# A two-layer hybrid trunk with eight experts: slot matrices made together, activations split per two blocks, the first expert weight tile split in the mixer

## The chip, the cores and the metric

The kernel runs on one core of a Trainium2 chip. The metric is the device time of one execution in microseconds (us). The engines that matter here are TensorE (PE, matmuls; PEld is its weight load), VectorE (DVE), ScalarE (ACT) and SyncE (SP), which issues the loads of weights. Each engine takes its instructions in the order in which they stand in its own list, and waits where an operand is not ready.

## What is computed

Two layers over 256 latent and 256 context tokens of width 1024. A layer is a norm, three parallel attention branches merged by gates, an output projection with a residual, a second norm and a feed-forward part. In layer 0 that is a dense SwiGLU; in layer 1 it is a mixture of eight experts of which each latent token uses two. Cut to the part that the change touches, with each token's rows gathered, passed through the expert and scattered back:

```python
def moe_swiglu(h, w_router, w_gu, w_dn):
    hf = h.reshape(n, D)
    logits = (hf @ w_router).astype(jnp.float32)
    top_logit, top_e = lax.top_k(logits, TOP_K)          # 2 of 8
    top_w = jax.nn.softmax(top_logit, axis=-1)
    ...
    xb = hf[src_tok].reshape(n_blocks, EXPERT_ROW_BLOCK, D)
    yb = lax.map(lambda a: swiglu(a[0], w_gu[a[1]], w_dn[a[1]]), (xb, block_expert))
    yb = yb.reshape(n_rows, D) * row_w[:, None].astype(h.dtype)
    return jax.ops.segment_sum(yb, src_tok, num_segments=n).reshape(B, L, D)

def swiglu(h, w_gu, w_dn):                               # w_gu: 1024 x 5632, w_dn: 2816 x 1024
    gate, up = jnp.split(h @ w_gu, 2, axis=-1)
    return (jax.nn.silu(gate) * up) @ w_dn
```

## The kernel before

All weights are fp32 in memory and are used as pairs of fp16: a tile `raw` of 128x2048 (1 MiB) is loaded by SP into a ring of raw buffers, ACT makes the high half (`wh<-raw`, line 269) and DVE the low half (`wl<-raw,wh`, line 266; `split`). Every product is three matmuls (high by high, high by low, low by high). The pairs live in a ring of three buffers (`WB = 3`, `new_parts`), so the split of a tile waits until the matmuls of the tile three places before have ended.

Each expert has room for 96 tokens (`CAP`) and 33 weight tiles. **Gate/up** are 22 of them, in 11 blocks `b` of two tiles: a tile is 48 matmuls of 96 columns (lines 332 to 334) into an accumulator `pa` (four buffers); behind a block ACT takes the Silu and DVE the product (`ht`, 128x192), which ACT and DVE split again (`hdh`, `hdl`). **Down** are the other 11 tiles: 44 steps `j` of three matmuls of 512 columns (lines 1300 to 1302) into `pg` (two buffers).

What an expert needs of the tokens is made by `gather`: from the slot numbers `posm` and weights `wsel` of the router, DVE makes a 0/1 matrix `P` (two instructions, line 1220), PE transposes it (line 1224; ACT copies it to `PT`, needed at the end to scatter), multiplies it by the weights (line 1228; DVE makes `wsl` of it, lines 1230 and 1231), and PE gathers the tokens' rows `hn` in 32 matmuls (line 1239, into two `pa` and two `pb` buffers), which ACT casts into `xg` (line 1241). Expert 0's is called in front of the experts; that of expert e+1 is called in the down phase of expert e (`j == 12`, `next_slots`). After experts 2, 5, 6 and 7 `combine` scatters the finished outputs back (line 1316) and DVE adds them to `xT`.

Ahead of the experts stands `route`: the second norm of layer 1, transposes of the normed tokens to `hn`, router logits, top 2, slots. The first three expert tiles are loaded early: tile 0 in the mixer's first part (into a buffer of the pool `px`), tiles 1 and 2 behind the mixer; the first two are split inside `route` (lines 1162 and 1203 for the high halves). The mixer's last part is the output projection (`out_chunk`): 8 chunks `d`, of which 0 to 3 are made for all latent tokens and 4 to 7 for each half of the tokens; behind each chunk DVE adds it to the residual `xT`, ACT squares it (`sq`) and DVE adds the squares (`acc`), whose sum over a half of the tokens starts the norm (lines 523 and 524).

The order on each engine comes from a scheduler that places instructions by dependences and its own times; `behind(...)` holds the instructions in its block back until the named ones have been issued on the same engine.

Of the kernel before, what the change touches and what calls it, by code (L numbers as in the profile page):

```python
# [17 lines left out]
D = 1024  # L18
KD = 8
NTOK = 512  # L20
NLAT = 256
# [228 lines left out]
def trunk(tc, A, out):  # L250
# [349 lines left out]
    def mixer(pool, i, ada_q, nrm, nxt, first=None):  # L600
# [444 lines left out]
        w = [W("wout2"), W("wout3")]  # L1045
        for p, c in enumerate(halves):
# [72 lines left out]
    ahead = [px.tile([128, 2048], FT, tag="raw3", bufs=1, name=nm("raw")) for _ in range(1)]  # L1119
# [20 lines left out]
    def route(pool):  # L1140
# [20 lines left out]
        with behind(nrm.end):  # L1161
            hi0 = S.activation(first[0][0], ahead[0], AF.Copy, scale=WS)
# [39 lines left out]
        with behind(e_):  # L1202
            S.activation(first[1][0], ahead[1], AF.Copy, scale=WS)
# [7 lines left out]
        with behind(V.tensor_tensor(wsel[:, :, :, 1], ex, wsel[:, :, :, 0], op=OP.subtract)):  # L1211
            for t in range(2):
                issued[0] = hi0, stt(first[t][1], ahead[t], WS, first[t][0], OP.mult, OP.subtract)

    def gather(pool, pos_e, w_e, slots):


        P = pool.tile([128, 2, CAP], F16, tag="P", bufs=2, name=nm("P"))
        for t in range(2):
            V.tensor_scalar(P[:, t], slots[:, :CAP], pos_e(t), None, op0=OP.is_equal)  # L1220
        PT = pool.tile([CAP, NLAT], F16, tag="PT", bufs=6, name=nm("PT"))
        pt = pb([128, D], F16)
        for t in range(2):
            T.transpose(pt[:CAP, 128 * t:128 * t + 128], P[:, t], ident16)
        S.copy(PT, pt[:CAP, :NLAT])
        pw = pb([128, 2])[:CAP]
        for t in range(2):
            T.matmul(pw, P[:, t], w_e(t), start=(t == 0), stop=(t == 1))
        wsl = pool.tile([CAP, 2], FT, tag="wsl", bufs=4, name=nm("wsl"))
        V.tensor_copy(wsl, pw)  # L1230
        V.tensor_scalar(wsl[:, 0:1], wsl[:, 0:1], wsl[:, 1:2], 1.0 / (WS * PSC), op0=OP.add, op1=OP.mult)
        xg = pool.tile([128, KD, 2, CAP], F16, tag="xg", bufs=2, name=nm("xg"))
        for j in range(2):
            for h in range(2):
                ps = (pb if h else pa)([128, 4, CAP])
                for k in range(4):
                    for t in range(2):
                        kk = 4 * h + k
                        T.matmul(ps[:, k], hn[j][:, t, 128 * kk:128 * kk + 128], P[:, t],  # L1239
                                 start=(t == 0), stop=(t == 1))  # L1240
                S.copy(xg[:, 4 * h:4 * h + 4, j], ps)
        return wsl, xg, PT

    def expert(pool, wsl, xg, tile_of, jobs, meanwhile, last=lambda *y: None, halves=(lambda *y: None,) * 2):
# [14 lines left out]
        for b in range(11):  # L1259
# [177 lines left out]
```

## Time and profile before

| | us |
|---|---|
| median of three executions | 1776.98 |
| lowest, highest | 1776.41, 1782.14 |
| the profiled execution | 1779.86 |
| its span, first to last instruction | 1777.8 |
| PE busy (share of the span) | 1649.0 (93%) |
| DVE busy | 1357.8 (76%) |
| ACT busy | 1040.6 (59%) |
| expert weight loads | 264 of 1 MiB |

The share of busy time is an average over parts with different limits: the experts are the last 700 us, and there DVE and ACT are far busier than the mean. A timeline row is: start, duration, engine, line, operation, output and inputs, and in brackets the idle time of the engine ahead of it and what ended that. The step from one start to the next tells the cost of an instruction better than its duration, since neighbours overlap. [...]

### The profile page before, as it was taken

Reading aid. Unit: us, or ns where it says so; the run is one execution under the profiler, and the core shown is the slowest. Engines: PE = TensorE matmul, PEld = TensorE weight load, DVE = VectorE, ACT = ScalarE, POOL = GpSimd, SP = SyncE. Lnnn points to the kernel's source line nnn. Section 1 sums busy time; section 2 is a strip of 40 time slices with the busy share of each in tenths; the row PEclk is TensorE's granted clock in tenths of the full one; section 3 lists DMA queues with packets and bytes.
Section 4 is the critical chain, followed back from the end, with each engine's and each line's share of the span. In section 5 each row is a group of like instructions: output and inputs, shape, how many; then the busy total and the mean of one; then the engine's idle time right before and its main releaser. Section 6 shows DMA issues by size and latency. Waiting matters only on the chain. (4 is left out here: it accounts for less than half of the span.)

```text
span 1777.8 us, 37905 instructions
## 1 busy us (share of the span) xinstructions
PE 1649.0 (93%) x16157; PEld 1086.9 (61%) x16157; DVE 1357.8 (76%) x1972; ACT 1040.6 (59%) x1399; POOL 1.3 (0%) x7
## 2 busy tenths in 40 slices
PE   5999899999999999999879988999899989998986
PEld 2554345446644444457646877686868686878684
DVE  4577656455886554547787779999989999989997
ACT  3456646343422322224666558888878888878785
POOL 0000000000000000000000000000000000000000
PEclk9999899999999999999988999999999999999998
DMA  9253488452365445534536669999999999999990
GB/s 388 101 153 88 109 250 225 134 192 96 138 224 207 168 161 177 182 112 159 160 84 158 194 262 366 416 410 410 417 400 385 408 422 408 418 387 396 390 391 26
DMA packets 149921, 451.94 MB, mean 254 GB/s; under 512 B 92144, under 2 KB 95344, under 8 KB 103024
## 3 DMA queue, kind: packets, MB, share of 16 engines
q1 hardware_dynamic: 148768, 448.50, 69.1%
q8 instruction: 128, 2.10, 0.5%
q10 hardware_dynamic: 976, 0.94, 0.2%
q14 instruction: 49, 0.40, 0.1%
HBM read 427.38 MB, written 1.05 MB: 241 GB/s over the span
## 5 line engine op out<-in xcount | busy, mean ns | idle before, releaser
L266 DVE SCALAR_TENSOR_TENSOR wl<-raw,wh 128x2048 f16<-128x2048 f32 (+1 forms) x476 | 820.5, 1735 | 52.7 <-ACT wh L269 50.7
L269 ACT ACTIVATE wh<-raw 128x2048 f16<-128x2048 f32 (+1 forms) x474 | 684.9, 1463 | 262.3 <-PE pa L333 92.6
L334 PEld LDWEIGHTS <-wl 128*128 128x128 f16 x4346 | 426.9, 98 | 183.0 <-DVE wl L266 66.9
L332 PEld LDWEIGHTS <-wh 128*128 128x128 f16 x4346 | 428.3, 99 | 131.3 <-issue 17.7
L333 PEld LDWEIGHTS <-wh 128*128 128x128 f16 x4346 | 427.4, 98 | 115.6 <-issue 8.7
L334 PE MATMUL pa<-xg,wl 128*128 128x96 f16 x2816 | 374.4, 207 | 42.9 <-DVE wl L266 42.9
L332 PE MATMUL pa<-xg,wh 128*128 128x96 f16 x2816 | 373.2, 206 | 1.0 <-ACT wh L269 1.0
L333 PE MATMUL pa<-xg,wh 128*128 128x96 f16 x2816 | 373.2, 206 | 0.1
L332 PE MATMUL pg<-hh,wh 128*128 128x512 f16 (+1 forms) x512 | 170.0, 332 | 5.7 <-ACT gt L972 2.7
L332 PE MATMUL pa<-hh,wh 128*128 128x512 f16 (+1 forms) x480 | 167.5, 355 | 6.1 <-ACT hh L552 6.1
L333 PE MATMUL pa<-hl,wh 128*128 128x512 f16 (+1 forms) x480 | 169.3, 354 | 1.3 <-DVE hl L266 1.3
L334 PE MATMUL pg<-hh,wl 128*128 128x512 f16 (+1 forms) x512 | 169.3, 331 | 0.7 <-DVE wl L266 0.7
L333 PE MATMUL pg<-hl,wh 128*128 128x512 f16 (+1 forms) x512 | 169.8, 332 | 0.0
L334 PE MATMUL pa<-hh,wl 128*128 128x512 f16 (+1 forms) x480 | 169.2, 353 | 0.0
L266 DVE SCALAR_TENSOR_TENSOR scr<-raw,cb 128x1024 f16<-128x1024 f32 x64 | 78.3, 1224 | 77.4 <-DMA raw<-in_ada 76.2
L1301 PE MATMUL pg<-wl,hdh 128*96 128x512 f16 x352 | 133.4, 379 | 1.0
L1302 PE MATMUL pg<-wh,hdl 128*96 128x512 f16 x352 | 133.4, 379 | 0.0
L1300 PE MATMUL pg<-wh,hdh 128*96 128x512 f16 x352 | 133.2, 379 | 0.0
L266 DVE SCALAR_TENSOR_TENSOR pn<-P,sml,pn 128x512 f16<-128x512 f32 (+1 forms) x96 | 60.9, 659 | 34.1 <-ACT pn L269 33.4
L269 ACT ACTIVATE pn<-P,sml 128x512 f16<-128x512 f32 (+1 forms) x96 | 59.1, 647 | 39.9 <-DMA pt<-pn 31.6
L913 ACT ACTIVATE P<-pa,sml 128x512 f32<-128x512 f32 (+1 forms) x96 | 58.1, 612 | 31.7 <-DVE sml L911 22.1
L269 ACT ACTIVATE hdh<-ht 128x192 f16<-128x192 f32 x88 | 31.9, 362 | 66.6 <-DVE ht L260 66.6
(250 smaller groups left out, 1919.3 us busy)
## 6 DMA issues: line engine op xcount, KB each, us to landing
raw<-in_wm SPq DMA_DIRECT2D x264, 1024.0 KB, 7.7
raw<-in_ws SPq DMA_DIRECT2D x52, 1024.0 KB, 4.8
raw<-in_ada SPq DMA_DIRECT2D x48, 1024.0 KB, 5.2
raw<-in_ws SPq DMA_DIRECT2D x18, 768.0 KB, 5.0
raw<-in_ws SPq DMA_DIRECT2D x16, 704.0 KB, 4.1
raw<-in_ws SPq DMA_DIRECT2D x16, 640.0 KB, 4.1
raw<-in_ws SPq DMA_DIRECT2D x4, 832.0 KB, 11.5
xT<-in_xt SPq DMA_DIRECT2D x4, 512.0 KB, 6.4
```

Source lines behind the costliest of these rows:

```text
L266: return V.scalar_tensor_tensor(o, a, s, b, op0=op0, op1=op1, **kw)
L269: h = S.activation(hi, src, AF.Copy, scale=scale)
L332: T.matmul(ps, sh, mh, start=first, stop=False)
L333: T.matmul(ps, sh, ml, start=False, stop=False)
L334: T.matmul(ps, sl, mh, start=False, stop=last)
L913: S.activation(P[t], ps[t], AF.Exp, bias=nb[:, t:t + 1], scale=sc, accum_out=sums[:, t:t + 1])
L1300: T.matmul(py, hdh[:, f], w[0][:, c], start=begin, stop=False)
L1301: T.matmul(py, hdh[:, f], w[1][:, c], start=False, stop=False)
L1302: T.matmul(py, hdl[:, f], w[0][:, c], start=False, stop=end)
```

## The change

Three things are changed. `gather` is divided: `slot_matrices` makes `P`, `PT` and `wsl`, first for expert 0 alone and then for experts 1 to 7 at once, held behind the low half of tile 2 (`behind(*lo)`); there are two DVE instructions of 128x672 for `P`, two copies for `PT` (96x1024 and 96x768) and one reduction with one scaling for `wsl`; what is left of `gather` is the 32 matmuls and the four casts, at the place of before. In the gate/up loop `ht` holds two blocks, and one split of 128x384 follows every second block; the eleventh block is split alone. The first expert tile is no longer loaded into a buffer of its own early in the layer; it is loaded and split in the mixer, after the loads of the output projection's last two tiles; the router then splits tiles 1 and 2, and tile 3 is loaded ahead as well. The ring of raw buffers keeps its size of twelve.

```diff
@@ mixer
         w = [W("wout2"), W("wout3")]
+        if last:
+            presplit.append(split_w(load_raw("wm", 0), 2048, step=2048))
         for p, c in enumerate(halves):
             for d in range(4, 8):
                 out_chunk(w[d // 2 - 2], d, c)
...
-    ahead = [px.tile([128, 2048], FT, tag="raw3", bufs=1, name=nm("raw")) for _ in range(1)]
+    presplit = []
@@ route
-            hi0 = S.activation(first[0][0], ahead[0], AF.Copy, scale=WS)
+            hi0 = S.activation(presplit[1][0], ahead[0], AF.Copy, scale=WS)
...
-            S.activation(first[1][0], ahead[1], AF.Copy, scale=WS)
+            S.activation(presplit[2][0], ahead[1], AF.Copy, scale=WS)
...
             for t in range(2):
-                issued[0] = hi0, stt(first[t][1], ahead[t], WS, first[t][0], OP.mult, OP.subtract)
-
-    def gather(pool, pos_e, w_e, slots):
-
-
-        P = pool.tile([128, 2, CAP], F16, tag="P", bufs=2, name=nm("P"))
+                lo[:] = [stt(presplit[1 + t][1], ahead[t], WS, presplit[1 + t][0], OP.mult, OP.subtract)]
+            issued[0] = hi0, lo[0]
+
+    def slot_matrices(pool, es, pos, w, slots):
+
+
+        n = len(es)
+        P = pool.tile([128, 2, n, CAP], F16, tag=f"P{n}", bufs=1, name=nm("P"))
         for t in range(2):
-            V.tensor_scalar(P[:, t], slots[:, :CAP], pos_e(t), None, op0=OP.is_equal)
-        PT = pool.tile([CAP, NLAT], F16, tag="PT", bufs=6, name=nm("PT"))
-        pt = pb([128, D], F16)
-        for t in range(2):
-            T.transpose(pt[:CAP, 128 * t:128 * t + 128], P[:, t], ident16)
-        S.copy(PT, pt[:CAP, :NLAT])
-        pw = pb([128, 2])[:CAP]
-        for t in range(2):
-            T.matmul(pw, P[:, t], w_e(t), start=(t == 0), stop=(t == 1))
-        wsl = pool.tile([CAP, 2], FT, tag="wsl", bufs=4, name=nm("wsl"))
-        V.tensor_copy(wsl, pw)
-        V.tensor_scalar(wsl[:, 0:1], wsl[:, 0:1], wsl[:, 1:2], 1.0 / (WS * PSC), op0=OP.add, op1=OP.mult)
+            sh = [128, n, CAP]
+            V.tensor_tensor(P[:, t], slots[:, None, :CAP].to_broadcast(sh), pos(t)[:, :, None].to_broadcast(sh),
+                            op=OP.is_equal)
+        PT = pool.tile([CAP, n, NLAT], F16, tag=f"PT{n}", bufs=1, name=nm("PT"))
+        for a in range(0, n, 4):
+            m = min(4, n - a)
+            pt = pb([128, 4, NLAT], F16)
+            for e in range(m):
+                for t in range(2):
+                    T.transpose(pt[:CAP, e, 128 * t:128 * t + 128], P[:, t, a + e], ident16)
+            S.copy(PT[:, a:a + m], pt[:CAP, :m])
+        pw = pb([128, n, 2])[:CAP]
+        for e in range(n):
+            for t in range(2):
+                T.matmul(pw[:, e], P[:, t, e], w(t)[:, e, :], start=(t == 0), stop=(t == 1))
+        wsl = pool.tile([CAP, n], FT, tag=f"wsl{n}", bufs=1, name=nm("wsl"))
+        V.tensor_reduce(wsl, pw, axis=AX.X, op=OP.add)
+        V.tensor_scalar(wsl, wsl, 1.0 / (WS * PSC), None, op0=OP.mult)
+        return [(wsl[:, e:e + 1], PT[:, e], lambda t, e=e: P[:, t, e]) for e in range(n)]
+
+    def gather(pool, P):
+
         xg = pool.tile([128, KD, 2, CAP], F16, tag="xg", bufs=2, name=nm("xg"))
...
@@ expert
-            t_ = pool.tile([128, 2, CAP], FT, tag="ht", bufs=3, name=nm("ht"))
+            if b % 2 == 0:
+                t4 = pool.tile([128, 4, CAP], FT, tag="ht", bufs=2, name=nm("ht"))
+            t_ = t4[:, 2 * (b % 2):2 * (b % 2) + 2]
             S.activation(t_, ps[:, :, 0], AF.Silu, scale=US)
-            f = slice(2 * b, 2 * b + 2)
             mul(t_, t_, ps[:, :, 1])
-            later.append(lambda f=f, t_=t_: split(hdh[:, f], hdl[:, f], t_, US * AS))
+            if b % 2 or b == 10:
+                n, f = 2 + 2 * (b % 2), slice(2 * b - 2 * (b % 2), 2 * b + 2)
+                later.append(lambda n=n, f=f, t4=t4: split(hdh[:, f], hdl[:, f], t4[:, :n], US * AS))
@@ the experts
-        raw_slots.extend([(px, "raw3", 1), (mr, "raw2", 5)])
-        ahead = ahead + [new_raw() for _ in range(2)]
...
+        raw_slots.append((mr, "raw2", 6))
+        ahead = [load_raw("wm", t * 128 * 2048) for t in range(1, 4)]
...
         with behind(issued[0][0]):
-            g = slots_of(0)
+            slots = matrices(0, 1)
+            xg = gather(pool, slots[0][2])
+        with behind(*lo):
+            slots += matrices(1, NE)
...
             def next_slots():
                 with behind(*issued[0]):
-                    return slots_of(e + 1)
+                    return gather(pool, slots[e + 1][2])
```

How this moves instructions is seen in the lists of three engines.

PE, the making of expert 2's inputs. Before, it stands in the down phase of expert 1, among the 512-column matmuls into `pg`; one row of each kind is shown, and 30 more gather matmuls (line 1239) follow ahead of the L1302:

```order
L1301 MATMUL pg_12877<-wl_12931,hdh_11613 96x512
L1224 LDWEIGHTS P_12934
L1224 MATMUL pb_12938<-ident_74,P_12934 96x128
L1228 LDWEIGHTS P_12934
L1228 MATMUL pb_12942<-wsel,P_12934 96x2
L1239 LDWEIGHTS hn_9835
L1239 MATMUL pa_12949<-P_12934,hn_9835 128x96
...
L1302 MATMUL pg_12877<-wh_12930,hdl_11614 96x512
```

After, half of it stands in expert 1's gate/up, among the 96-column matmuls into `pa` (the gathers are now on line 1253):

```order
L334 MATMUL pa_12301<-xg_11442,wl_12359 128x96
L332 LDWEIGHTS wh_12418
L332 MATMUL pa_12415<-xg_11442,wh_12418 128x96
L333 LDWEIGHTS wh_12418
L333 MATMUL pa_12415<-xg_11442,wh_12418 128x96
L1253 LDWEIGHTS hn_9840
L1253 MATMUL pb_12941<-P_10118,hn_9840 128x96
...
L1253 MATMUL pb_12961<-P_10118,hn_9841 128x96
L334 LDWEIGHTS wl_12419
L334 MATMUL pa_12415<-xg_11442,wl_12419 128x96
```

The run of 13 gather matmuls now stands right ahead of the first matmul of a tile that needs its low half (`wl`), and the transposes and slot weights are gone from both phases. By the whole list the down phases of experts 0 to 6 hold 32, 16, 0, 16, 16, 0 and 0 gather matmuls now (32 each before); those of experts 2 and 5 hold 16 of the matmuls that scatter (12 before).

DVE, gate/up of expert 0. Before, a product or a split of 192 columns stands behind every weight split:

```order
L266 SCALAR_TENSOR_TENSOR wl_10672<-raw_10669,wh_10671 128x2048
L260 TENSOR_TENSOR ht_10551<-ht_10551,pa_10440 128x192
L266 SCALAR_TENSOR_TENSOR wl_10726<-raw_10723,wh_10725 128x2048
L266 SCALAR_TENSOR_TENSOR hdl_10113<-ht_10551,hdh_10112 128x192
L266 SCALAR_TENSOR_TENSOR wl_10786<-raw_10783,wh_10785 128x2048
```

After, two products and one split of 384 columns stand among four weight splits:

```order
L266 SCALAR_TENSOR_TENSOR wl_10592<-raw_10589,wh_10591 128x2048
L260 TENSOR_TENSOR ht_10474<-ht_10474,pa_10363 128x192
L266 SCALAR_TENSOR_TENSOR wl_10646<-raw_10643,wh_10645 128x2048
L266 SCALAR_TENSOR_TENSOR wl_10706<-raw_10703,wh_10705 128x2048
L260 TENSOR_TENSOR ht_10474<-ht_10474,pa_10477 128x192
L266 SCALAR_TENSOR_TENSOR wl_10760<-raw_10757,wh_10759 128x2048
L266 SCALAR_TENSOR_TENSOR hdl_10159<-ht_10474,hdh_10158 128x384
```

One instruction in eight is gone, and none of the columns.

ACT, the end of the mixer and the start of expert 0. Before, the squares of the output projection's chunks follow one another, and at the start the cast of the last gathered piece stands behind the split of tile 2 (`raw_9849`):

```order
L508 ACTIVATE sq_9517<-xT 128x128
L508 ACTIVATE sq_9546<-xT 128x128
L508 ACTIVATE sq_9549<-xT 128x128
...
L1241 CAST xg_10071<-pb_10082 128x4x96
L269 ACTIVATE wh_10215<-raw_9849 128x2048
L1241 CAST xg_10071<-pb_10102 128x4x96
L269 ACTIVATE wh_10269<-raw_10267 128x2048
L269 ACTIVATE wh_10329<-raw_10327 128x2048
```

After, the split of tile 0 (`raw_9567`) stands ahead of the squares of chunk 3, and the casts stand together; `raw_9857` is tile 3, and the two copies of `PT` stand ahead of tile 4:

```order
L508 ACTIVATE sq_9516<-xT 128x128
L269 ACTIVATE wh_9569<-raw_9567 128x2048
L508 ACTIVATE sq_9545<-xT 128x128
...
L1254 CAST xg_10077<-pb_10088 128x4x96
L1254 CAST xg_10077<-pb_10108 128x4x96
L269 ACTIVATE wh_10309<-raw_9857 128x2048
L1234 COPY PT_10121<-pb_10122 96x1024
L1234 COPY PT_10121<-pb_10132 96x768
L269 ACTIVATE wh_10366<-raw_10364 128x2048
```

The low half of tile 0 moves on DVE in the same way, to in front of the sums of chunk 3's squares. On PE the first two of the 14 transposes of experts 1 to 7 stand behind the first matmul of tile 1, the other twelve 13 matmuls later, and the 14 slot-weight matmuls 30 behind those.

## Rows read from the trace of the kernel before

**Rows 1.** Stretches; busy PE, PEld, DVE, ACT, POOL; PE clock, DMA share, GB/s.

```profile
1054.00:1060.00 6.00, 4.37 (x48) 2.59 (x45) 5.42 (x28) 3.57 (x9) 0.00 (x0) 0.99 0.60 247
1060.00:1074.00 14.00, 8.16 (x94) 6.26 (x94) 12.11 (x45) 12.89 (x22) 0.00 (x0) 0.51 0.29 85
1150.00:1200.00 50.00, 45.87 (x851) 39.79 (x849) 49.08 (x37) 42.13 (x37) 0.00 (x0) 1.00 1.00 407
1200.00:1250.00 50.00, 48.45 (x571) 34.94 (x569) 47.03 (x35) 41.06 (x35) 0.00 (x0) 1.00 1.00 410
```

**Rows 2.** Waits, 1090 to 1730 us: total, times, longest.

```profile
PE pa L334 <- DVE wl L266: 42.1, 146, 0.9
ACT wh L269 <- PE pg L1302: 22.8, 30, 1.3
...
ACT wh L269 <- DMA raw<-in_wm: 9.7, 13, 1.0
```

**Rows 3.** SyncE's waits, 1090 to 1730 us; and its loads, from the page.

```profile
SPq L304 <- DVE wl L266: 205.1, 86, 4.0
...
raw<-in_wm SPq DMA_DIRECT2D x264, 1024.0 KB, 7.7
```

**Rows 4.** Timeline of DVE, gate/up of expert 1: start, duration, instruction.

```profile
1176.03 0.34 DVE L260 TENSOR_TENSOR ht<-ht,pa 128x192 f32<-128x192 f32 x1
1176.29 2.28 DVE L266 SCALAR_TENSOR_TENSOR wl<-raw,wh 128x2048 f16<-128x2048 f32 x1
1178.49 0.35 DVE L266 SCALAR_TENSOR_TENSOR hdl<-ht,hdh 128x192 f16<-128x192 f32 x1
1178.77 2.28 DVE L266 SCALAR_TENSOR_TENSOR wl<-raw,wh 128x2048 f16<-128x2048 f32 x1
```

**Rows 5.** Groups of DVE instructions by shape, from 1090 us on: busy, mean ns.

```profile
L260 DVE TENSOR_TENSOR raw<-raw,pb 128x512 f32<-128x512 f32 x4 | 2.5, 682 | 0.8 <-PE pb L533 0.8
```

**Rows 6.** Timeline of PE, gate/up of expert 1.

```profile
1175.70 0.21 PE L333 MATMUL pa<-xg,wh 128*128 128x96 f16 x1
1176.16 0.22 PE L334 MATMUL pa<-xg,wl 128*128 128x96 f16 x1 [0.26 <-DVE wl L266]
```

**Rows 7.** Timeline of PE, down phase of expert 1.

```profile
1220.95 0.38 PE L1301 MATMUL pg<-wl,hdh 128*96 128x512 f16 x1
...
1222.47 0.50 PE L1239 MATMUL pb<-P,hn 128*128 128x96 f16 x8
1222.81 0.38 PE L1302 MATMUL pg<-wh,hdl 128*96 128x512 f16 x1
```

**Rows 8.** Timeline of PE, down phase of expert 0.

```profile
1135.43 0.38 PE L1302 MATMUL pg<-wh,hdl 128*96 128x512 f16 x1
...
1136.98 0.38 PE L1300 MATMUL pg<-wh,hdh 128*96 128x512 f16 x1
...
1137.63 0.38 PE L1300 MATMUL pg<-wh,hdh 128*96 128x512 f16 x1
...
1139.08 0.38 PE L1301 MATMUL pg<-wl,hdh 128*96 128x512 f16 x1
```

**Rows 9.** Timeline of ACT, end of the mixer and start of expert 0.

```profile
1042.86 0.51 ACT L508 ACTIVATE sq<-xT 128x128 f32<-128x128 f32 x2 [1.09 <-DVE xT L266]
...
1073.14 1.91 ACT L269 ACTIVATE wh<-raw 128x2048 f16<-128x2048 f32 x1
1074.96 0.47 ACT L1241 CAST xg<-pb 128x384 f16<-128x384 f32 x1
1077.17 3.90 ACT L269 ACTIVATE wh<-raw 128x2048 f16<-128x2048 f32 x2 [1.74 <-issue]
```

**Rows 10.** Timeline of DVE, end of the mixer and start of expert 0.

```profile
1047.09 0.29 DVE L263 TENSOR_TENSOR acc<-acc,sq 128x128 f32<-128x128 f32 x1 [0.43 <-ACT sq L508]
...
1083.79 2.28 DVE L266 SCALAR_TENSOR_TENSOR wl<-raw,wh 128x2048 f16<-128x2048 f32 x1
```

**Rows 11.** Timeline of PE, end of the mixer.

```profile
1041.97 0.27 PE L334 MATMUL pa<-mh,wl 128*128 128x256 f16 x1
```

More of the change, by code (lines that the diff above doesn't have):

```diff
@@ L1238, in gather @@
                         kk = 4 * h + k
-                        T.matmul(ps[:, k], hn[j][:, t, 128 * kk:128 * kk + 128], P[:, t],
-                                 start=(t == 0), stop=(t == 1))
+                        T.matmul(ps[:, k], hn[j][:, t, 128 * kk:128 * kk + 128], P(t), start=(t == 0), stop=(t == 1))
                 S.copy(xg[:, 4 * h:4 * h + 4, j], ps)
-        return wsl, xg, PT
+        return xg
     def expert(pool, wsl, xg, tile_of, jobs, meanwhile, last=lambda *y: None, halves=(lambda *y: None,) * 2):
@@ L1339, in trunk @@
           tc.tile_pool(name="mr", bufs=1, reuse_waits="tile") as mr):
-        raw_slots.extend([(px, "raw3", 1), (mr, "raw2", 5)])
-        ahead = ahead + [new_raw() for _ in range(2)]
-        for t, raw in enumerate(ahead):
-            nc.sync.dma_start(raw, dram("wm", t * 128 * 2048, 2048))
-        first = [new_parts() for _ in range(2)]
-        route(pool)
+        raw_slots.append((mr, "raw2", 6))
+        ahead = [load_raw("wm", t * 128 * 2048) for t in range(1, 4)]
+        presplit.extend(new_parts() for _ in range(2))
+        lo = []
+        route(pool, lo)
         raw_slots.extend([(st, "hh", 1), (st, "hl", 1)])
@@ L1349, in moe_w, with matrices @@
         def moe_w(e, t):
-            if e == 0 and t < len(first):
-                return first[t]
-            if e == 0 and t < len(ahead):
-                return split_w(ahead[t], 2048, step=2048)
+            if e == 0 and t < len(presplit):
+                return presplit[t]
+            if e == 0 and t <= len(ahead):
+                return split_w(ahead[t - 1], 2048, step=2048)
             return split_w(load_raw("wm", (33 * e + t) * 128 * 2048), 2048, step=2048)
-        def slots_of(e):
-            return gather(pool, lambda t: posm[:, t, e:e + 1], lambda t: wsel[:, t, e, :], slot)
-        ys, jobs, late = [], [], lambda: None
+        def matrices(a, b):
+            return slot_matrices(pool, range(a, b), lambda t: posm[:, t, a:b], lambda t: wsel[:, t, a:b], slot)
+        jobs, ys, late = [], [], lambda: None
         with behind(issued[0][0]):
-            g = slots_of(0)
+            slots = matrices(0, 1)
+            xg = gather(pool, slots[0][2])
+        with behind(*lo):
+            slots += matrices(1, NE)
         for e in range(NE):
-            wsl, xg, PT = g
+            wsl, PT, _ = slots[e]
             if e == NE - 1:
@@ L1372, in next_slots @@
                 with behind(*issued[0]):
-                    return slots_of(e + 1)
-            yh, yl, g, late = expert(pool, wsl, xg, lambda t: moe_w(e, t), jobs, next_slots, late)
+                    return gather(pool, slots[e + 1][2])
+            yh, yl, xg, late = expert(pool, wsl, xg, lambda t: moe_w(e, t), jobs, next_slots, late)
             ys.append((yh, yl, PT))
@@ L1404, in tile_of @@
                         return split_w(raw, 2048)
-                    wsl, xg, PT = gather(pool, lambda t: pe[:, t:t + 1], lambda t: we[:, t, :], slot2)
+                    (wsl, PT, P), = slot_matrices(pool, range(1), lambda t: pe[:, t:t + 1], lambda t: we[:, t:t + 1],
+                                                  slot2)
+                    xg = gather(pool, P)
                     yh, yl, _, late = expert(pool, wsl, xg, tile_of, [], lambda: None)
```

4 lines of the change are left out of this document (2 added, 2 removed).

## The prediction, made before the changed kernel was run

> **What bounds the kernel now.** I read first the busy time by stretch, then the waits of the expert stage, then single rows of one expert's two phases, and last the start of expert 0.
>
> Behind 1090 us the experts run back to back to the end of the span, and two engines take turns as the bound. A stretch that is almost all gate/up (1150 to 1200) has DVE busy 49.08 of 50 us; one that holds a whole down phase (1200 to 1250) has PE at 48.45 [rows 1]. The waits say the same: TensorE waits 42.1 us in 146 pieces for the low halves that DVE makes (gate/up), and ACT waits 22.8 us for the last down matmuls to give a weight buffer back (down). ACT's waits for a load are 9.7 us in all [rows 2], and SyncE waits 205.1 us, in 86 pieces, for DVE to free a raw buffer before it may issue the next load [rows 3]. So the ring of loaded tiles is full and the loads run ahead, although the DMA engines are busy all the time.
>
> *Gate/up.* DVE has no gap. A 2048-column split starts at 1176.29, the next instruction at 1178.49, so it costs 2.20 us; the 192-column ones around it cost 0.26 (1176.03 to 1176.29) and 0.28 (1178.49 to 1178.77), 0.27 in the mean [rows 4]. Each tile has one split and one 192-column instruction: 2.47 us. PE runs 48 matmuls of 0.0425 us (eight take 0.34 [rows 7]), 2.04 us, and then waits for the low half: from 1175.70 to 1176.16 the step is 0.46 where it should be 0.04 [rows 6]. PE thus has about 0.42 us to spare per tile, some 9 us in the 22 tiles of one expert.
>
> *Down.* PE issues a 512-column matmul every 0.217 us (three steps from 1136.98 to 1137.63 [rows 8]); 132 of them are 28.6 us, and nothing hides what stands among them. In expert 1 one L1301 starts at 1220.95 and the L1302 behind it at 1222.81: 1.86 less one step, 1.64 us for the transposes, the slot weights, their hand-over and the 32 gather matmuls of the next expert [rows 7]. Expert 0 pays twice: 1136.98 less 1135.43 less a step is 1.33, and 1139.08 less 1137.63 less a step is 1.23 [rows 8]; 2.57 together. The 1.64 stands once in each of experts 1 to 6, with the same rows.
>
> **The change part by part.** The sum is made against the profiled execution, 1779.86 us (span 1777.8 and 2.1 around it). It stands 0.16% above the median of 1776.98.
>
> *1. One activation split per two blocks.* Per expert eleven 192-column splits become five of 384 and one of 192, on ACT and on DVE. ACT has room in gate/up; DVE has none, so DVE's saving is time. From the two costs of rows 4, a column costs (2.20 − 0.27) / (2048 − 192) = 1.04 ns and an instruction 0.07 us besides. A 384-column split then costs 0.47 instead of twice 0.27: 0.07 saved, 5 times 8 experts: −2.8 us. No row has a 384-column split; the nearest are the 128x192 one, 0.35 us from start to end [rows 4], and a 128x512 addition with 682 ns [rows 5]: 1.04 ns a column between them too, which is the slope taken. Bounds: 0 (a bigger split that makes something else late) and −3.5 (the five joins at 0.087).
> The trace puts the part of a DVE instruction that does not grow with its columns at 0.07 us. [...]
>
> *2. Slot matrices at once, gather alone.* The 14 transposes, 14 slot-weight matmuls and their copies leave the down phases. The 32 gather matmuls stay, but now hang only on the token rows and P, both ready early, and the order shows where they go: in experts 1, 3, 4 half of them (16) and in 2, 5, 6 none are left in the down phase, the others stand in gate/up, where PE waits for DVE anyway. Expert 0 keeps all 32, in one run. Sixteen cost 0.68, thirty-two 1.36 (0.34 per eight [rows 7]). So expert 0 gives 2.57 − 1.36 = 1.2; 1, 3 and 4 give 1.64 − 0.68 = 0.96 each; 2 and 5 give 1.64 less four combine matmuls that move in (0.11 each, half the columns of a down matmul): 1.2 each; 6 gives 1.64 less about 0.35, because ACT now casts four gathered pieces in a row ahead of tile 26 and PE may wait for it: 1.3. Together −7.8. DVE needs 11 times 2.20 = 24.2 us for a down phase's splits, so it is not late when PE takes 29.5 instead of 30.5. In gate/up 16 gather matmuls in one tile are 0.68 against 0.42 of slack; the 0.26 left over falls on the next tile, and that has slack too. Bounds: −1.9 (only what is not a matmul goes: 1.64 − 1.36 = 0.28, seven times) and −11.5 (all of 2.57 and six times 1.5).
>
> *3. The first weight tile in the mixer.* Removed: a load early in layer 1 and its split in the router, where it was hidden. Added: a load, an ACT split (1.9) and a DVE split (2.2) in the output projection. The order puts the ACT split ahead of the squares of chunk 3. It wants a weight buffer that the matmuls of chunk 3 free; their last starts at 1041.97 [rows 11]. ACT then has the split until about 44.1 and the two squares behind it, which stood at 1042.86 [rows 9]. DVE has its split until 46.3, and behind it three additions, two residuals and more additions at 0.2 to 0.27 each; the sum over the first half of the tokens, which ended at 1047.09 + 0.29 [rows 10], is ready some 1.0 us later, and the norm, router and top-2 all hang on it. +1.0, bounds 0.5 and 1.5. On SyncE the load stands behind the last projection loads, which wait for nothing new; tiles 1 to 3 stand behind a load that now waits for tile 0's split (about 1046.5), and are wanted 20 us after that, with loads landing 7.7 us after their issue [rows 3].
>
> *4. The start of expert 0.* Gain: tile 2's ACT split (1073.14, 1.91) no longer stands before the last gather cast (1074.96) [rows 9]; that cast comes 1.9 earlier and PE ends tile 0, which frees a buffer for tile 3, earlier by 1.9 less the 1.0 of part 3. Loss: DVE makes P of seven experts in two instructions of 672 columns, 0.77 each at the slope above, in front of tile 3's split. PE's order has the first two transposes of these after one matmul of tile 1, so PE stands about 1.7 us until the second P is there (near 1077.9), and has 28 small matmuls (1.4) more in that tile. ACT copies them out (0.95 and 0.77) ahead of tile 4's split, which also waits for tile 1's buffer. Followed through, tile 5's low half, which starts at 1083.79 [rows 10], starts near 1085.4 to 1086. Everything behind it keeps DVE's pace. So 3 and 4 net +2.0; bounds 0 (the gain covers the rest) and +4.5 (P waits and the two copies add instead of overlapping).
>
> Sum: −2.8 − 7.8 + 2.0 = −8.6: the profiled run at 1771.3, the median at 1768.4.
>
> **The rivals.**
> *A. The gather stays dear.* The hoisted matmuls push gate/up as much as they spared in down: wherever the low half is waited for, PE's spare 0.42 is already spent on the next tile's start. Then only the 0.28 per expert is won: −2.8 − 1.9 + 2.0 = −2.7, 1774.3. Against it: 146 waits with 42.1 us [rows 2]. Chance 0.11.
>
> *B. The start costs far more.* [...] Chance 0.09.
>
> *C. The loads are the bound.* The DMA share is 1.00 at 407 to 410 GB/s [rows 1]; if these engines set the pace, a shorter down phase only makes ACT wait for tiles. The 264 tiles then need what they need now and only the +2.0 is left: 1779.0. Against it: SyncE waits for buffers, not the reverse [rows 2, 3]; twelve raw tiles at 2.47 us are 29.6 us, of which a load takes 7.7. [...] Chance 0.05.
>
> *D. Slower: gathers block the accumulators.* In gate/up a block's accumulator and two of the four gathered pieces share the four pa buffers. A piece is freed by an ACT cast, and on ACT that cast stands behind a 1.9 us weight split which may itself wait for PE. If the next block then finds no buffer, PE stands for that split: 1.9 less the 0.42 of slack, 1.5 for each of two pieces, 3.0 per expert, six experts: +17.8, and 1786.2 in all. It ends slower than before from 1.4 us per expert, slower by over 0.3% from 2.3. Against it: a block lives about 5 us, so two buffers are usually free. Chance 0.09.
>
> That the early tile brings nothing by itself is part of the forecast: three weight buffers hold tiles 0 to 2, and tile 3 waits for PE to end tile 0 as it did [rows 9].
>
> **How the numbers follow.** A measurement here tells 0.3%, 5.3 us. Forecast 0.66, with its own spread of about 4 us: nearly all of it below 1771.65, 0.61, the rest within 0.3%. A, B and C lie within 0.3% (0.01 of A beyond): 0.24. D is slower: 0.09. So faster 0.62, same 0.29, slower 0.09. The range goes from 1763.5 (−13.5: parts 1 and 2 at their far ends, −15, with +1.5 for the start) to 1776.5, which takes in A and B.
>
> **What would show it.** Part 1: in gate/up a pair of blocks takes 9.80 us of DVE instead of 9.87. Part 2: down phases shorter by 1.2, 1.0, 1.2, 1.0, 1.0, 1.2 and 1.3 us in experts 0 to 6, with no transposes among them; PE's wait for low halves shrinks from 42.1 by the 6 to 7 us of gathers moved there. Parts 3 and 4: the first statistics matmul of the second norm 1 us later and tile 5's low half 2 us later. The forecast is wrong if PE waits for pa buffers or ACT casts in gate/up, if ACT waits for loads by more than 10 us, or if the low clock lasts past tile 1.

## The result: 0.5% faster

The changed kernel takes 1770.29 us (median of 7 executions, 1769.57 to 1772.54) against 1777.81 for the kernel before (1776.41 to 1784.17). The ratio on record is 0.9946, with a 95% interval of 0.9932 to 0.996; the two medians by themselves give 0.9958. The forecast was 1768.4 in a range of 1763.5 to 1776.5.

The two profiled executions have spans of 1777.8 and 1768.3 us, 9.5 apart. Not all of that need be the change: the parts ahead of it, in which PE runs the same matmuls in the same order, differ by chance. One matmul of the output projection, the same one in both lists, serves as a **mark** from here on; the last down matmul of expert 7 is the other end. Timeline of PE, before and then after:

```profile
1044.87 0.22 PE L334 MATMUL pg<-mh,wl 128*128 128x128 f16 x1
```

```profile
1759.52 0.38 PE L1302 MATMUL pg<-wh,hdl 128*96 128x512 f16 x1
```

```profile
1043.69 0.22 PE L334 MATMUL pg<-mh,wl 128*128 128x128 f16 x1
```

```profile
1748.77 0.38 PE L1318 MATMUL pg<-wh,hdl 128*96 128x512 f16 x1
```

From the mark to the last down matmul it is 714.65 us before and 705.08 after: 9.57 less. The 1.2 us by which the mark itself comes earlier, and 1.2 us at the other end, in the write of the output, cancel and are no part of the change. In the thirteen profiled executions of this study the mark stands between 1041.2 and 1052.1. Where an experiment is about 1 us, the steps from the mark are therefore compared, and the times of whole executions stand beside them.

One thing behind the mark differs by chance as well. At the start of expert 0 the clock granted to PE, as a share of the full one, is 0.5 for a stretch [rows 1], 13.6 us long before and 17.0 after, and the place where it rises to 1.00 is not the same in every execution: 28.7 us behind the mark before, 30.4 after. In seven of the thirteen executions (the changed kernel and six of the experiments) PE, ACT and DVE run the same instructions in the same order from the mark to the low half of expert 0's tile 5. In five of these the clock rises 30.3 to 30.4 us behind the mark and that low half starts at 41.1; it starts at 41.65 where the clock rises at 32.1 (the run with all gathers in one place of gate/up) and at 40.77 where it rises at 29.5 (the run with splits per four blocks). So up to 0.9 us of a difference in the first 41 us can be the clock alone.

Stretches of after, to set against [rows 1], and ACT's, PE's and DVE's waits of after from 1090 to 1715 us, against [rows 2]:

```profile
1060.00:1074.00 14.00, 8.30 (x93) 6.48 (x94) 12.21 (x45) 12.01 (x21) 0.00 (x0) 0.50 0.35 135
1150.00:1200.00 50.00, 46.49 (x882) 40.89 (x881) 49.08 (x34) 41.38 (x33) 0.00 (x0) 1.00 1.00 414
1200.00:1250.00 50.00, 48.94 (x592) 35.66 (x588) 47.39 (x29) 42.34 (x34) 0.00 (x0) 1.00 1.01 421
```

```profile
PE pa L334 <- DVE wl L266: 34.9, 95, 1.0
ACT wh L269 <- PE pg L1318: 34.4, 44, 1.3
ACT ht L1285 <- PE pa L334: 24.0, 34, 0.8
...
ACT wh L269 <- DMA raw<-in_wm: 3.4, 5, 0.7
```

The two bounds are the same as before: DVE with 49.08 of 50 in gate/up, as it was, and PE with 48.94 where a down phase lies (48.45 before). PE waits for low halves 34.9 us instead of 42.1. The gathers that now fill the gaps are only one part of that: over stretches of like length the run below that holds them in the down phases has 36.8, and the one that undoes the joins 36.0. Waits for loads fell from 9.7 to 3.4.

The table takes the 9.57 apart. The steps are read from the timelines: the start of the second norm's statistics (DVE, line 526), of the low half of expert 0's tile 5, and of the first and last down matmul of each expert. Where the length of an expert is told below, it runs from the low half of its tile 0 to that of the next expert.

| step | before | after | change | forecast |
|---|---|---|---|---|
| mark to the norm's statistics | 4.00 | 4.98 | +0.98 | +1.0 |
| statistics to tile 5 of expert 0 | 34.92 | 36.11 | +1.19 | +1.0 |
| tile 5 to the end of the last down phase | 675.73 | 663.98 | −11.75 | −10.6 |
| of that: down phases 0 to 7, first to last matmul and one step of 0.217 | 247.2 | 239.2 | −8.0 | −7.8 |
| of that: gate/up and the changes between phases | 428.5 | 424.8 | −3.8 | −2.8 |

**Gate/up after** (timeline of DVE, expert 1): one period of two blocks, from one `ht` to its like.

```profile
1175.20 0.34 DVE L260 TENSOR_TENSOR ht<-ht,pa 128x192 f32<-128x192 f32 x1
1175.47 6.68 DVE L266 SCALAR_TENSOR_TENSOR wl<-raw,wh 128x2048 f16<-128x2048 f32 x3
...
1184.54 0.55 DVE L266 SCALAR_TENSOR_TENSOR hdl<-ht,hdh 128x384 f16<-128x384 f32 x1
1185.01 0.34 DVE L260 TENSOR_TENSOR ht<-ht,pa 128x192 f32<-128x192 f32 x1
```

From 1175.20 to 1185.01 it is 9.81 us; four tiles at the 2.47 of [rows 4] are 9.88. The 384-column split costs 0.47 (1184.54 to 1185.01), as worked out.

**Down after** (timeline of PE). In expert 0, against [rows 8], the gathers stand in one run, between L1318 at 1135.89 and L1316 at 1137.47; in expert 1, against [rows 7], two short runs are left, of which this is the first:

```profile
1135.89 0.38 PE L1318 MATMUL pg<-wh,hdl 128*96 128x512 f16 x1
...
1137.47 0.38 PE L1316 MATMUL pg<-wh,hdh 128*96 128x512 f16 x1
```

```profile
1219.52 0.38 PE L1316 MATMUL pg<-wh,hdh 128*96 128x512 f16 x1
1219.74 0.55 PE L1253 MATMUL pb<-P,hn 128*128 128x96 f16 x9
1220.12 0.38 PE L1317 MATMUL pg<-wl,hdh 128*96 128x512 f16 x1
```

1.58 less one step of 0.217 is 1.36 in expert 0 (2.57 before); 1220.12 less 1219.52 less a step is 0.38 in expert 1, and 0.30 more stands at 1222.50, 0.68 together (1.64 before). No transpose is among them. From first to last matmul the down phases of experts 0 to 6 are shorter by 1.5, 1.0, 1.0, 1.0, 1.0, 1.3 and 1.3 us, where 1.2, 1.0, 1.2, 1.0, 1.0, 1.2 and 1.3 were forecast.

### The profile page after: what moved, and what is told of

It is laid out like the page before. It is cut to its first block, busy times and chain, and to the rows that moved or that the text cites. A ratio compares the mean times of both kernels' runs of the same rounds, so it can differ in the third digit from the quotient of the medians.

```text
span 1768.3 us, 37807 instructions
## 1 busy us (share of the span) xinstructions
PE 1644.8 (93%) x16157; PEld 1085.5 (61%) x16157; DVE 1351.6 (76%) x1908; ACT 1038.1 (59%) x1354; POOL 1.3 (0%) x7
## 5 line engine op out<-in xcount | busy, mean ns | idle before, releaser
L1318 PE MATMUL pg<-wh,hdl 128*96 128x512 f16 x352 | 133.4, 379 | 0.0
L1316 PE MATMUL pg<-wh,hdh 128*96 128x512 f16 x352 | 132.3, 379 | 0.0
L333 PE MATMUL pg<-dl,wh 128*128 128x512 f16 (+1 forms) x198 | 70.4, 355 | 0.0
```

The source lines that it names most:

```text
L333: T.matmul(ps, sh, ml, start=False, stop=False)
L1316: T.matmul(py, hdh[:, f], w[0][:, c], start=begin, stop=False)
L1318: T.matmul(py, hdl[:, f], w[0][:, c], start=False, stop=end)
```

## The experiments

### The joins alone: splits of one block again

```diff
-            if b % 2 == 0:
-                t4 = pool.tile([128, 4, CAP], FT, tag="ht", bufs=2, name=nm("ht"))
-            t_ = t4[:, 2 * (b % 2):2 * (b % 2) + 2]
+            t_ = pool.tile([128, 2, CAP], FT, tag="ht", bufs=3, name=nm("ht"))
...
-            if b % 2 or b == 10:
...
+            later.append(lambda f=f, t_=t_: split(hdh[:, f], hdl[:, f], t_, US * AS))
```

> The changed kernel with its activation splits undone: one of 128x192 behind each block again. Forecast's theory (in gate/up VectorE has no gap, so its instructions are the time): 40 joins undone at 0.07 us, +2.8 us over the changed kernel's 1770.3, 1773.1; a pair of blocks takes 9.87 us of VectorE instead of 9.80. Rival (PE or the loads pace gate/up once the gathers stand there): no change, 1770.3.

Measured: 1773.33 us (ratio to before 0.9957, 0.994 to 0.9974); from the mark to the last down matmul 708.6, +3.5 over the changed kernel. Each expert is longer, by 0.34 to 0.54. Of expert 1's 0.45, 0.35 lies in gate/up between the low halves of tiles 3 and 24 (52.49 against 52.14 us), which is five joins at 0.07; the other 0.1 comes at the change to the down phase. The rival falls. The term was right in kind and 0.7 us short.

### The gathers: held in the down phase

```diff
-            if j == 12:
-                res = meanwhile()
...
-            T.matmul(py, hdh[:, f], w[1][:, c], start=False, stop=False)
+            m_ = T.matmul(py, hdh[:, f], w[1][:, c], start=False, stop=False)
+            if j == 12:
+                with behind(m_):
+                    res = meanwhile()
```

> The changed kernel with the 32 gather matmuls of each next expert held on TensorE behind a matmul of the down phase, where before had them; slot matrices stay made at once. Forecast's theory (matmuls in down are path, in gate/up they are free): 16 more in experts 1, 3, 4 (0.68 each) and 32 more in 2, 5, 6 (1.36 each), less 3 scatter matmuls fewer in 2 and 5 (0.33 each): +5.4 us, 1775.7. Rival A (the hoisted matmuls cost gate/up what they spare in down): no change, 1770.3.

Measured: 1776.47 us (0.998, 0.9967 to 0.9992); 710.5 from the mark, +5.4. Timeline of PE, down phase of expert 1; the gathers are back, without the transposes:

```profile
1228.08 0.38 PE L1315 MATMUL pg<-wl,hdh 128*96 128x512 f16 x1
1228.29 0.50 PE L1253 MATMUL pa<-P,hn 128*128 128x96 f16 x8
...
1229.65 0.38 PE L1319 MATMUL pg<-wh,hdl 128*96 128x512 f16 x1
```

1.57 less a step is 1.36 in one place, twice the 0.68 that the changed kernel leaves. Rival A falls: what leaves the down phase is not paid in gate/up. And of the 9.57 us more than half hangs on the place that the scheduler found for these matmuls, not on making the slot matrices at once.

### The gathers: all of them in one place of gate/up

```diff
-            if j == 12:
-                res = meanwhile()
...
             if jobs and b > 1:
                 jobs.pop(0)()
+            if b == 6:
+                res = meanwhile()
```

> The changed kernel with the gather of the next expert called behind block 6 of gate/up instead of step 12 of down; no down phase holds a gather matmul any more, and those of experts 2 and 5 hold 8 scatter matmuls instead of 16. Forecast's theory (TensorE has 0.42 us to spare in each of 22 tiles): expert 0 gives 1.36, experts 1, 3 and 4 give 0.68 each, 2 and 5 give 0.88 each: -5.2 us, 1765.1. Rival (32 matmuls in one place are 1.36 against the 0.42 of one tile, and three weight buffers do not cover that): the lump costs VectorE 0.9 us per expert, seven times, and the time stays at 1770 to 1771.

Measured: 1771.98 us (0.9953, 0.9935 to 0.997); 706.2 from the mark, 1.1 *more* than the changed kernel. The down phases did get shorter, by 4.7 us in all (28.85 us in expert 1 instead of 29.44), but from tile 3 to tile 22 each of seven experts got longer by 0.9 (expert 1: 47.88 us instead of 47.00), 6.2 in all; from tile 22 to tile 3 of the next expert it is 5.6 less. The other 0.55 stands at the start of expert 0 and is no part of the edit: it is the late clock told of under the result. The rival named the size; its reason was wrong. Timelines of ACT and of DVE, expert 1:

```profile
1191.20 0.47 ACT L1254 CAST xg<-pa 128x384 f16<-128x384 f32 x1
...
1192.30 0.51 ACT L1254 CAST xg<-pb 128x384 f16<-128x384 f32 x1
1192.67 3.75 ACT L269 ACTIVATE wh<-raw 128x2048 f16<-128x2048 f32 x2
```

```profile
1193.52 0.34 DVE L260 TENSOR_TENSOR ht<-ht,pa 128x192 f32<-128x192 f32 x1
1194.65 4.49 DVE L266 SCALAR_TENSOR_TENSOR wl<-raw,wh 128x2048 f16<-128x2048 f32 x2 [0.79 <-ACT wh L269]
```

It is not PE that is late. The split at 1192.67 is that of tile 16, which takes the buffer of tile 13, and PE had issued the last matmul of tile 13 before the gathers (timeline of PE):

```profile
1190.44 0.21 PE L334 MATMUL pa<-xg,wl 128*128 128x96 f16 x1
```

Four casts in a row, the first and the last of them shown, 1.47 us from 1191.20 to 1192.67, stand on ACT ahead of that weight split, and DVE waits 0.79 us for it.

### The gathers in four pieces

```diff
+        steps = []
+        res = meanwhile(steps)
...
+            if steps and b in (3, 5, 7, 9):
+                with behind(*issued[0]):
+                    steps.pop(0)()
```

Here `gather` puts its four groups of eight matmuls and one cast into `steps` instead of issuing them.

> The changed kernel with the next expert's gather made in four pieces (8 matmuls and one ACT cast each) behind blocks 3, 5, 7 and 9 of gate/up. Theory after the run with the gather behind block 6 (what cost 0.8 us per expert there was not the matmuls but four ACT casts in a row ahead of one weight split, for which VectorE then waits): with one cast at a time nothing is lost in gate/up and the down phases give 4.7 us as they did there: from the mixer's end to the last down matmul 700.4 us against the changed kernel's 705.1, total 1765.6. Rival (the matmuls themselves do not fit into gate/up): no gain, 705 and 1770. Rival (the loads pace the experts): no gain either, and ACT's waits for loads grow.

Measured: 1769.12 us (0.9924, 0.9908 to 0.9939); 700.2 from the mark, 4.9 less than the changed kernel. Timelines of ACT and of DVE at one piece in expert 1, where the cast at 1191.33 delays nobody:

```profile
1191.33 0.48 ACT L1254 CAST xg<-pb 128x384 f16<-128x384 f32 x1
1191.70 1.91 ACT L269 ACTIVATE wh<-raw 128x2048 f16<-128x2048 f32 x1
```

```profile
1191.63 2.27 DVE L266 SCALAR_TENSOR_TENSOR wl<-raw,wh 128x2048 f16<-128x2048 f32 x1
...
1194.10 2.27 DVE L266 SCALAR_TENSOR_TENSOR wl<-raw,wh 128x2048 f16<-128x2048 f32 x1
```

DVE goes from 1191.63 to 1194.10 in 2.47 us. From tile 3 to tile 22 expert 1 takes 47.02 us again, and in these stretches of all experts DVE waits only once for ACT by more than 0.1 us, 0.23 in expert 0.

This run divides the matmuls as well as the casts, so it does not tell by itself which of the two cost 0.8 us where all gathers stood in one place. Expert 2 tells, in that run and in the changed kernel: in both PE has the same 13 gather matmuls, and 3 more behind them, among the tiles of its gate/up (timelines of PE, that run and then the changed kernel; DVE, that run):

```profile
1268.83 0.72 PE L1253 MATMUL pa<-P,hn 128*128 128x96 f16 x13
```

```profile
1289.54 0.72 PE L1253 MATMUL pa<-P,hn 128*128 128x96 f16 x13
```

```profile
1272.45 2.29 DVE L266 SCALAR_TENSOR_TENSOR wl<-raw,wh 128x2048 f16<-128x2048 f32 x1 [0.80 <-ACT wh L269]
```

In that run three casts stand on ACT from 1269.37 to 1270.48, ahead of the split for which DVE then waits 0.80, and tiles 3 to 22 take 47.89 us; in the changed kernel the casts are elsewhere, DVE does not wait there, and the tiles take 47.00. The casts are thus shown as the cause: in these runs matmuls in gate/up were free as far as their casts came one at a time.

### The first tile: loaded and split as before

```diff
-        if last:
-            presplit.append(split_w(load_raw("wm", 0), 2048, step=2048))
...
+    ahead = [px.tile([128, 2048], FT, tag="raw3", bufs=1, name=nm("raw"))]
...
-        raw_slots.append((mr, "raw2", 6))
-        ahead = [load_raw("wm", t * 128 * 2048) for t in range(1, 4)]
+        raw_slots.extend([(px, "raw3", 1), (mr, "raw2", 5)])
```

> The changed kernel with the first weight tile loaded into its own buffer and split in the router as before. Theory one (the mixer pays 1.0 us for that split and the start of expert 0 gets it back, because tile 2's split need not be made among the gather casts and the copies of PT): statistics of the second norm 1.0 us earlier, tile 5's low half 0 to 0.4 us later than in the changed kernel, time 1770.3 to 1770.7. Rival (the split in the mixer is a plain loss): 1.0 us faster, 1769.3.

Measured: 1768.35 us (0.9942, 0.992 to 0.9963); 704.7 from the mark, 0.35 less than the changed kernel. The statistics come at 4.00 again, and from there to tile 5 it is 36.84 instead of 36.11. So the mixer pays 0.98 for the early split and the start gives 0.73 back: theory one in the main, with a loss of a quarter of a microsecond or a little more left, which a whole execution can't show. Tile 5 stands 0.26 earlier behind the mark than in the changed kernel, not 0 to 0.4 later as theory one had it.

### The first tile in quarters

```diff
-            presplit.append(split_w(load_raw("wm", 0), 2048, step=2048))
+            raw0 = load_raw("wm", 0)
+            presplit.append(new_parts())
         for p, c in enumerate(halves):
             for d in range(4, 8):
+                if last and p == 0:
+                    q = slice(512 * (d - 4), 512 * (d - 4) + 512)
+                    split(presplit[0][0][:, q], presplit[0][1][:, q], raw0[:, q], WS)
```

> The changed kernel with the first tile's split in the mixer cut into four quarters of 512 columns between the half-chunks of the output projection. Theory (the mixer loses 1.0 us because 1.9 us of ACT and 2.2 us of VectorE stand in one piece ahead of squares and sums, while each half-chunk of 1.34 us leaves VectorE 0.8 us idle): the second norm's statistics come 4.2 us behind the mark instead of 4.98, -0.8 us, 1769.5. Rival (the weight buffer that the split waits for comes too late in any cutting): no change, 1770.3.

Measured: 1769.46 us (0.9926, 0.9912 to 0.994); the statistics come 4.24 behind the mark, 0.74 earlier than in the changed kernel, and 704.4 to the last down matmul, 0.66 less. The split of a whole tile on DVE in the changed kernel, and the quarters here (timelines of DVE):

```profile
1042.94 2.29 DVE L266 SCALAR_TENSOR_TENSOR wl<-raw,wh 128x2048 f16<-128x2048 f32 x1
1045.15 0.69 DVE L263 TENSOR_TENSOR acc<-acc,sq 128x128 f32<-128x128 f32 x3
```

```profile
1044.85 1.29 DVE L266 SCALAR_TENSOR_TENSOR wl<-raw,wh 128x512 f16<-128x512 f32 x2
1046.07 0.48 DVE L263 TENSOR_TENSOR acc<-acc,sq 128x128 f32<-128x128 f32 x2
...
1046.73 0.68 DVE L266 SCALAR_TENSOR_TENSOR wl<-raw,wh 128x512 f16<-128x512 f32 x1
1047.33 0.28 DVE L263 TENSOR_TENSOR acc<-acc,sq 128x128 f32<-128x128 f32 x1
```

The sums of squares (`acc`) come between the quarters, where in the changed kernel they waited behind 2.2 us.

### The transposes later

```diff
+        steps = [lambda a=a: copies(a) for a in range(0, n, 4)] + [weights]
+        if hold is None:
+            for f in steps:
+                f()
+        else:
+            hold.extend(steps)
...
+        jobs = [lambda f=f: held(f) for f in first_jobs]
```

`copies` holds the transposes and a copy to PT, `weights` the slot weights; `held` keeps them behind the last weight split and the last matmul issued, so that they stand behind blocks 2, 3 and 4 of expert 0.

> The changed kernel with the transposes, PT copies and slot weights of experts 1 to 7 held back to blocks 2 to 4 of expert 0's gate/up; P is still made at the start. Theory (at the start they stand in tile 1's matmuls and ahead of tile 4's split and delay it by about 1.2 us): tile 5's low half 39.9 us behind the mixer's end instead of 41.1, and 0.2 of it lost later to the copies in front of two weight splits: -1.0 us, 1769.3. Rival (the start is set by P on VectorE, or by tile 0): no change, 1770.3.

Measured: 1769.88 us (0.9931, 0.9916 to 0.9946); tile 5 is 39.7 behind the mark instead of 41.1, 1.4 less, and 0.4 of that is lost by the start of expert 1: 704.2 to the last down matmul, −0.85. The 1.4 is rather too small: the clock rose 32.1 us behind the mark here, 1.6 later than in the changed kernel, and the last matmul of tile 0 came 0.4 later. At the start of expert 0 the changed kernel's rows say why (timelines of ACT, DVE and PE, against [rows 9, 10]):

```profile
1074.08 0.48 ACT L1254 CAST xg<-pb 128x384 f16<-128x384 f32 x1 [0.96 <-PE pb L1253]
1076.37 1.91 ACT L269 ACTIVATE wh<-raw 128x2048 f16<-128x2048 f32 x1 [1.81 <-PE pa L334]
1078.18 1.69 ACT L1234 COPY PT<-pb 96x1024 f16<-96x1024 f16 x2
1080.38 1.91 ACT L269 ACTIVATE wh<-raw 128x2048 f16<-128x2048 f32 x1 [0.51 <-ACT PT L1234]
```

```profile
1082.32 2.29 DVE L266 SCALAR_TENSOR_TENSOR wl<-raw,wh 128x2048 f16<-128x2048 f32 x1 [1.44 <-PE pa L334]
...
1084.79 4.49 DVE L266 SCALAR_TENSOR_TENSOR wl<-raw,wh 128x2048 f16<-128x2048 f32 x2
```

```profile
1079.22 0.75 PE L1238 MATMUL pb<-wsel,P 128*96 128x2 f16 x14 [0.48 <-ACT PT L1234]
```

Tile 3's split ends at 1078.2. Two copies to PT (1.69 us) stand behind it; the slot-weight matmuls wait 0.48 for a buffer that the second copy frees, with tile 1's last four matmuls behind them; and tile 4's split (1080.38) waits for tile 1's weight buffer. DVE idles 1.44 us ahead of 1082.32.

### The three together

> The three together: gather in pieces, transposes late, first tile in quarters. If each is worth what its theory says and they do not meet in one place: -4.7 - 1.0 - 0.8 = -6.5, from the mixer's end to the last down matmul 698.6 us, total 1763.8. If the late transposes and the pieces meet in expert 0's blocks: 0.5 to 1 us less gain.

Measured: 1761.68 us (1759.21 to 1768.18), ratio to before 0.9896 (0.9878 to 0.9914); 697.5 from the mark, 7.6 less than the changed kernel and 17.2 less than before. It beats both kernels. Alone they gave 4.9, 0.85 and 0.66, 6.4 in all. Most of the surplus is at the start (statistics to tile 5 33.9 us, where late transposes alone gave 34.7), and it is the clock, not the parts helping each other: between these two points PE, ACT and DVE run the same instructions in the same order in both runs. The granted clock rose 24.6 us behind the statistics in this run and 27.1 behind them in the other, and the last matmul of tile 0 came 0.87 apart. The stretch between these two rises, in this run and then in the other:

```profile
1070.60:1073.10 2.50, 2.15 (x50) 2.04 (x48) 2.50 (x5) 0.48 (x1) 0.00 (x0) 1.00 0.92 269
```

```profile
1074.50:1077.00 2.50, 2.33 (x31) 2.20 (x29) 2.50 (x5) 0.48 (x1) 0.00 (x0) 0.50 0.78 262
```

### The three, with the first tile as before

> The version with gathers in pieces and late transposes, but the first weight tile loaded and split as in the kernel before. If the early split in the mixer is still worth its place when the transposes are gone from the start: 0.74 less in the mixer than the whole tile cost there, so against the version with quarters (697.5 from the mixer's end to the last down matmul) the mixer is 0.24 us shorter and the start 0.7 longer, 698.0. If the start no longer needs it: 697.2.

Measured: 1763.59 us (0.9907, 0.9883 to 0.9932); 698.5 from the mark. Mixer 4.00 against 4.23, start 34.98 against 33.86: the version with all three, which has the early split, takes 1.1 us less at the start for 0.23 more in the mixer. Not all of the 1.1 is the split. Behind the statistics the clock rose after 25.7 us here and after 24.6 there, and the last matmul of tile 0 started at 28.0 here and at 27.0 there. In the changed kernel and in the one with its first tile in quarters, which have the early split, the clock rose at 25.5 and 25.2, and that matmul started at 27.4. By these about 0.6 us of the 1.1 is left to the split, an estimate, and less the 0.23 some 0.4: what lost 0.35 in the changed kernel, in one piece, gains a little here, in quarters.

### Fewer raw buffers

```diff
-        raw_slots.append((mr, "raw2", 6))
+        raw_slots.append((mr, "raw2", 2))
```

> The changed kernel with eight buffers for loaded tiles instead of twelve. Forecast's theory (a tile lies loaded for some 17 us before it is split, four buffers fewer take 10 us of that away): no change within 0.5 us, from the mixer's end to the last down matmul 705.1. Rival C (the loads are the bound and the ring's depth carries them over the stretches in which VectorE is fast): ACT waits for loads in every expert and the time rises by more than 5 us.

Measured: 1770.08 us (0.9947, 0.9922 to 0.9973); 705.05 from the mark, as the changed kernel, and no wait for a load is among ACT's waits from 1090 to 1715 us. Rival C falls.

### Splits per four blocks

```diff
-            if b % 2 == 0:
-                t4 = pool.tile([128, 4, CAP], FT, tag="ht", bufs=2, name=nm("ht"))
-            t_ = t4[:, 2 * (b % 2):2 * (b % 2) + 2]
+            g0, gn = [(0, 4), (4, 4), (8, 2), (10, 1)][min(b // 4, 2) if b < 10 else 3]
+            if b == g0:
+                t4 = pool.tile([128, 8, CAP], FT, tag="ht", bufs=2, name=nm("ht"))
+            t_ = t4[:, 2 * (b - g0):2 * (b - g0) + 2]
...
```

> The changed kernel with its activation splits joined over four, four, two and one blocks (128x768, 128x768, 128x384, 128x192), and eleven raw buffers to make room. Theory (each join saves the fixed part of one VectorE instruction, 0.07 us): two more joins per expert, -1.1 us, 704.0 from the mixer's end to the last down matmul. Rival (the longer ACT split stands ahead of a weight split, and VectorE waits for that as it did behind the four casts): the joins cost more than they save, 706 or more.

Measured: 1771.31 us (0.9941, 0.992 to 0.9962), which tells nothing against 1770.29; from the mark 703.8, 1.3 less than the changed kernel. Of that 0.33 stands ahead of tile 5, where the clock rose earlier; the other 0.97 is 0.06 per join. One ACT split of 768 columns, unlike four casts, makes nobody wait (timeline of ACT, expert 1):

```profile
1181.81 0.84 ACT L269 ACTIVATE hdh<-ht 128x768 f16<-128x768 f32 x1 [0.88 <-DVE ht L260]
1182.56 0.31 ACT L1286 ACTIVATE ht<-pa 128x192 f32<-128x192 f32 x1
```

## Why the prediction was right, and where it was not

**The sum.** −8.6 was forecast, −9.57 is what the stretch from the mark lost, and −7.5 is the difference of the medians, in which the luck of the first 1040 us lies too.

**Part 1, the joins** (−2.8). Right in mechanism: DVE has no gap in gate/up (busy 49.08 of 50 us), the period of two blocks fell by the 0.07 that was worked out, and undoing it cost 3.5. The term is 0.7 short. Five times 0.07 per expert is there to the hundredth; what was left out is about 0.1 per expert at the change to the down phase. By the steps in the trace, 0.27 us for a split of 192 columns and 0.47 for one of 384, the part of a DVE instruction that does not grow with its columns is 0.07 us, an estimate; the splits per four blocks gave 0.06 per join.

**Part 2, the gather** (−7.8). Right, −8.0 by the down phases, and the expected +5.4 of the run that undid it came to the tenth. One thing in it was not seen. That gate/up has room was argued from PE's 0.42 us per tile; the room that runs out first is ACT's, ahead of a weight split, by four casts in a row. The changed kernel escapes this although its four casts stand in a row too, since they stand in the down phase, where DVE is not the bound (47.39 us busy from 1200 to 1250, PE 48.94): in expert 1 some 5 us behind the first down matmul at 1211.48 (timeline of ACT).

```profile
1216.88 0.46 ACT L1254 CAST xg<-pa 128x384 f16<-128x384 f32 x1
...
1217.97 0.50 ACT L1254 CAST xg<-pb 128x384 f16<-128x384 f32 x1
```

Expert 6's 0.35 was there, as forecast (one step of 0.33 us too long at 1644.43).

**Part 3, the mixer** (+1.0). Right: +0.98, of which 0.74 lies in the size of the pieces, as the quarters show.

**Part 4, the start** (+1.0 beyond part 3). The net is right, +1.19, but by luck, as two errors cancel, and the clock alone can move it by more than the 0.2 that is left. The step "that cast comes 1.9 earlier" failed: the last gather cast stands 30.4 us behind the mark (1074.08) where before it stood 30.1 [rows 9]; by that step, with part 3's 1.0 taken off, it should have stood 0.9 earlier. Tile 2's split is out of the way, but the cast then waits 0.96 us for the gather matmuls, which run at the lower clock until 1074 (0.50 in the stretch above). And the step "PE stands about 1.7 us until the second P is there" failed: the second P was begun at 1075.63, while PE was still at tile 0, and the first two transposes follow tile 0 at 1075.97 without a wait. The delay came from what was named third, the copies and the small matmuls ahead of tile 4's split.

**The rivals.** A falls by the held gathers, and by the gathers in pieces, which take 4.9 us more out of the same place. B: the start took 2.17 us more (0.98 and 1.19); no run shows the larger excess that the top of the range, 1776.5, takes in for B, and from 1075 us to the last down matmul the granted clock is 1.00. C: eight raw buffers do as well as twelve, and the version with all three moves the same bytes in 17.2 us less. The loads are not held to the rate of before either: from 1200 to 1250 us the trace of after shows 421 GB/s, where it was 410 [rows 1]. D did not happen, for no wait for a pa buffer by PE is among the waits; but its core, a cast and a weight split in each other's way on ACT, is what cost 0.8 to 0.9 us per expert when all gathers were called in one place.

## What to carry to other kernels

An engine's spare time was not one number here: PE and ACT both had room in gate/up, and 1.47 us of ACT work in one piece cost 0.8 us of the bound engine where the same work in four pieces cost 0.23 in one expert and next to nothing in the others. So cut what is moved into pieces smaller than the lead of the engine that feeds the bound, and read that lead from the wait behind it. A gain that hangs on where a scheduler puts instructions (5.4 of 9.6 us here) is worth writing out by hand, and an edit that loses a little in one surrounding (the early split, 0.35 us slower) can gain in another (some 0.4, an estimate). And before a surplus is put down to two edits that help each other, compare the granted clock of the two executions: here it made 0.87 us between the same instructions.

## What the runs showed of the hardware

The part ahead of the mark, with the same matmuls in the same order in all, took between 1041.2 and 1052.1 us in the profiled executions. Laid side by side, before and after differ there by 1.5 us in a single stretch, 981 to 989 us, in which the granted clock was 1.00 before and 0.62, then 0.95 after. The clock is not the whole of it: ahead of the mark it was at 0.5 for 44 to 58 us (54.6 both in before and in after), and the execution with the earliest mark and the one with the latest both had 51.2 us of that. What else moves the mark is open. In this kernel a difference of a few microseconds between two executions needs the steps of a stretch beside it, and the clock of that stretch.
